# Moving every large tile of a two-layer diffusion block to SBUF addresses that are multiples of 1024 bytes

## The chip, the cores and the metric

The kernel runs on one core of a Trainium2 chip. Five engines work side by side: TensorE (matrix products; PE in the profile, with its loads of the stationary operand listed apart as PEld), VectorE (DVE), ScalarE (ACT), GpSimd (POOL) and SyncE (SP), whose queue issues all the DMAs here. On-chip memory, the SBUF, has 128 partitions; a tile is a block of up to 128 partitions and lies at the same byte address in each of them. The metric is the device time of one execution in microseconds (us); the kernel before takes 1386.08 us in the median of three runs.

## The reference

One latent stream `x` of 512 tokens and one context stream of 256 tokens, 1024 features each, go through two layers: differential attention, then a gated short convolution. Each is followed by a SwiGLU feed-forward block (FFN) with an inner width of 2816.

```
for i in range(2):
    sh1, sc1, g1, sh2, sc2, g2 = split(silu(c) @ ada_w[i] + ada_b[i], 6)
    h  = rmsnorm(x, norm1_g[i]) * (1 + sc1) + sh1
    y  = diff_attention(h, hc, ...) if i == 0 else short_conv(h, ...)
    x  = x + g1 * y
    h2 = rmsnorm(x, norm2_g[i]) * (1 + sc2) + sh2
    a, b = split(h2 @ ffn_w_in[i], 2)
    x  = x + g2 * ((silu(a) * b) @ ffn_w_out[i])
return rmsnorm(x, final_g)
```

In the attention each head has two softmax maps, of which the second is subtracted with a learned weight. Only the latent stream is returned, so of the context only what the first attention reads of it is computed.

## The kernel before

Features lie on the partitions and tokens on the free axis. A float32 product runs as three passes in float32r: each operand is split into a rounded part (hi) and the rest (lo), and hi*hi, hi*lo and lo*hi add up in PSUM. Those are the three lines of `mm3` (L78, L79, L80 in the profile), which nearly all products pass through:

```
nc.tensor.matmul(ps, sh, mh, start=start, stop=False)
nc.tensor.matmul(ps, sh, ml, start=False, stop=False)
nc.tensor.matmul(ps, sl, mh, start=False, stop=stop)
```

A matmul has a stationary operand (128 by 128, mostly a block of weights, loaded anew for each matmul) and a moving operand (mostly 512 or 256 columns of activations, 4 bytes each, so 2048 or 1024 bytes of every partition). `load_w` fetches 128x1024 of weights by DMA (`raw`), ScalarE casts the hi part (L54), VectorE subtracts it to get lo (L55). A tile of weights holds eight blocks of 512 bytes.

The order of work is that of the program's text, as a scheduler has merged it: the first norm and the first head's projections (to about 110 us); eight heads of attention, each beside the next one's projections (`attend`, `proj_qk_steps`, `proj_v_steps`; to about 460 us); the FFN of layer 0 (`ffn_in`, tiles pa and pb from h2; `out_gemm`, tile po_fo0 from U); the short convolution (psc, psu, psb from h1; po_so from Y); the FFN of layer 1 (pa and pb from h3; po_fo1 from U) and the last norm.

**Where tiles lie.** Pools are stacked from both ends of a partition. On the left `const` (small constants) begins at byte 1152 and ends at 5728; on it stand the pools `wp` and `wp2` (weights), `ap` (attention), `lp`, `up0`, `up1` (the FFN's inner values, tiles uh and ul) and `yp` (tiles yh and yl). Everything in them has a size that is a multiple of 1024 bytes, so the large tiles all begin at 608 modulo 1024, as 5728 does. On the right, pools go down from byte 229344, which is 992 modulo 1024: `hp` (the first norm's output, hh, hl, ch, cl), `h2p`, `h1p` and `h3p` (the later norms' outputs), `xtp` (the residual stream) and `op` (tiles o, later the last eight blocks of the first FFN's inner values, there called u). These large tiles begin at 992 modulo 1024. Both 608 and 992 are 32 modulo 64. One pool, `ap2`, lies above `ap` and its small tiles, at 192 modulo 1024; it holds ada, araw, qt, kt, rcos, rsin, sw and rt, which VectorE, ScalarE, GpSimd and DMAs use in the attention. A block of weights begins at 608 or 96 modulo 1024.

Of the kernel before, what the change touches and what calls it, by code (L numbers as in the profile page):

```python
# [11 lines left out]
F32 = mybir.dt.float32  # L12
# [4 lines left out]
PSUM = bass.MemoryType.PSUM  # L17

P = 128
# [5 lines left out]
def block_kernel(  # L25
# [6 lines left out]
    """Features on partitions, tokens on the free axis, from the first norm to the last.  # L32

    A float32 product runs as three float32r passes: each operand is split exactly into a part
    rounded to float32r (hi) and the rest (lo), and hi*hi + hi*lo + lo*hi accumulate in PSUM.
    """
# [27 lines left out]
    def load_w(src, name, dst=None):  # L64
        """[n*128, cols] of weights (n*cols <= 1024) as (hi, lo), each [128, n, cols]."""
        n, ncol = src.shape[0] // P, src.shape[1]
        w = n * ncol
        raw = wp.tile([P, 1024], F32, tag="raw", name=f"raw_{name}")
        nc.sync.dma_start(
            raw[:, :w].rearrange("p (k c) -> p k c", c=ncol),  # L70
            src.rearrange("(k p) c -> p k c", p=P),
        )
        return tuple(
            t[:, :w].rearrange("p (k c) -> p k c", c=ncol) for t in split_w(raw, w, name, dst)
        )
# [6 lines left out]
    def gemm_block(ps, ws, mov):  # L82
        """ps[128 outputs, tokens] = w.T @ mov; ws the tiles of w by rows, mov a list of (hi, lo) by block."""
        n, k = len(mov), 0
        for wh, wl in ws:
            for i in range(wh.shape[1]):
                mm3(ps, wh[:, i, :], wl[:, i, :], mov[k][0], mov[k][1], k == 0, k == n - 1)
                k += 1
# [4 lines left out]
    # ---------------------------------------------------------------- constants, small vectors  # L93
    st1 = const.tile([P, P], F32, name="st1")
    st2 = const.tile([P, P], F32, name="st2")
    nc.vector.memset(st1, 0.0)
    nc.vector.memset(st2, 0.0)
    rows = lambda v: v.rearrange("(j p) -> j p", p=P)
    nc.sync.dma_start(st1[0:8, :], rows(c[0]))
    nc.sync.dma_start(st1[8:16, :], rows(c_ctx))  # L100
    nc.sync.dma_start(st1[16:64, :], rows(ada_b[0]))
    nc.sync.dma_start(st1[64:72, :], rows(norm1_g[0]))
# [5 lines left out]
    nc.vector.tensor_copy(ones_r, ones_f)  # L108
    mhalf = const.tile([P, 8], F32, name="mhalf")
    nc.vector.memset(mhalf, -0.5)  # L110

    # ---------------------------------------------------------------- pools of the first layer
# [4 lines left out]
    # what the last head doesn't use any more, in a pool of its own  # L117
# [7 lines left out]
    # places: first what is done with when the next pools land on it  # L125
# [16 lines left out]

    def load_ada0(k, hf):
        """Columns of block k of the first norm's shift and scale, half of the rows: [4 blocks of rows][s][128]."""
        raw = wp.tile([P, 1024], F32, tag="raw", name=f"raw_a{k}_{hf}")
        rv = raw.rearrange("p (k s c) -> p k s c", s=2, c=P)
        for s in range(2):
            nc.sync.dma_start(
                rv[:, :, s, :],
                ada_w[0, hf * 512:(hf + 1) * 512, s * D + k * P:s * D + (k + 1) * P]  # L150
                .rearrange("(k p) c -> p k c", p=P),
            )
        return raw

    # streams in natural layout, by blocks of 128 tokens
# [18 lines left out]
    # silu of both conditioning vectors; as stationary columns (hi, lo) of each  # L174
# [11 lines left out]
    # ---------------------------------------------------------------- first norm  # L186
    def spread(r, n, tag, name):
        """Columns r[128 tokens, n] as [128, n*128] in PSUM, the same on every partition."""
        rh = ap.tile([P, 4], F32R, tag="rh", name=f"rh{name}")[:, :n]
        rl = ap.tile([P, 4], F32, tag="rl", name=f"rl{name}")[:, :n]  # L190
        nc.vector.tensor_copy(rh, r)
        nc.vector.tensor_tensor(rl, r, rh.bitcast(F32), op=ALU.subtract)
        ps = psB.tile([P, 512], F32, tag=tag, name=f"spr{name}")[:, :n * P]
        for i, q in enumerate((rh.bitcast(F32), rl)):
            dg = ap.tile([P, 4, P], F32R, tag=f"dg{i}", bufs=1, name=f"dg{i}{name}")[:, :n, :]
            nc.gpsimd.tensor_tensor(
                dg, ident[:, None, :].to_broadcast([P, n, P]), q[:, :, None].to_broadcast([P, n, P]),
                op=ALU.mult,
            )
            nc.tensor.matmul(ps, ones_r, dg.rearrange("p a b -> p (a b)"), start=(i == 0), stop=(i == 1))  # L200
        return ps

    def nat_rstd(src, tag, name):
        """1/rms of natural-layout tokens, spread over the partitions."""
# [27 lines left out]
    # modulation of the first norm, both streams: [block of D][shift, scale][latent, context]  # L232
# [28 lines left out]
    # the first group's values and the first head's queries and keys, block by block of the norms' output  # L261
# [25 lines left out]
    for k in range(DB):  # L287
# [12 lines left out]
        for t in range(TB):  # L300
            # two accumulations share a bank: the first one's start clears it for both
            mm3(
                vps[0][:, t * 256:(t + 1) * 256],
                hx[k][0][:, t * P:(t + 1) * P], hx[k][1][:, t * P:(t + 1) * P],
                wh[:, 256:512], wl[:, 256:512], k == 0 and t % 2 == 0, k == DB - 1 and t % 2 == 1,
            )
# [23 lines left out]
    # the other small vectors  # L330
# [15 lines left out]
    # lambda  # L346
# [9 lines left out]
    # ---------------------------------------------------------------- adaLN vectors on VectorE  # L356
    def ada_steps(l, j, pool, ps_pool, spread_sum):
        """mod[l][:, 8j:8j+8]: one modulation vector of the latent stream, in steps."""
        acc = pool.tile([P, D], F32, tag="ada", bufs=1, name=f"ada{l}_{j}")
        for k in range(DB):  # L360
# [3 lines left out]
            if not spread_sum:  # L364
                # VectorE is the busy one beside attention
# [21 lines left out]
        # sums over the partitions, on every partition; the diagonal blocks are the columns  # L387
# [21 lines left out]
    # ---------------------------------------------------------------- attention  # L409
# [18 lines left out]
    def halves_to(dst, src, both):  # L428
        """Moves a map's 64 rows of (hi, lo) where the score products want them."""
        for m in range(2):  # L430
            s = src[64 * m:64 * m + 64]
            for d in range(2):
                o = dst[m][64 * d:64 * d + 64]
                nc.sync.dma_start(
                    o.bitcast(F32), (s if both else s[:, d, :]).bitcast(F32)
                )

    def finish_q(h, ps):
        """Per map [hi; hi] and [lo; lo], the scores' scale (a power of two) folded in."""
# [7 lines left out]
    def finish_k(h, ps, psc):  # L447
        """Per map [hi; lo], latent keys first."""
# [55 lines left out]
    def attend(h, between, after=None):  # L504
# [4 lines left out]
        for pr in range(2):  # L509
# [6 lines left out]
            for s in range(2):  # L516
# [19 lines left out]
                # both maps over the first one's denominator, which the sub-norm takes up  # L536
# [26 lines left out]
    def subnorm(h, den, t0, t1):  # L563
        """O is den * o, so eps is scaled by den^2 under the root."""
# [18 lines left out]
    # first group and head: projected already  # L583
# [4 lines left out]
    # ---------------------------------------------------------------- norms and products after it  # L588
# [51 lines left out]
    def pair(pool, i, name):  # L640
        """(hi, lo) in place i of pool."""
# [3 lines left out]
    def wo_steps():  # L645
        """The first heads' part of the output projection, in the place of the norm's output."""
# [34 lines left out]
    for h in range(NH):  # L681
        # beside a head: the next one's queries and keys, part of the next group's values, or
        # the output projection
# [43 lines left out]
    def sqrt_ahead(k):  # L727
        """Has the square root's table loaded while the products before a norm still run."""
# [6 lines left out]
    class beside:  # L735
        """The second norm's first half runs beside the end of attention, in places of its early values."""
# [8 lines left out]
    # the FFN's first weights, in places of the first heads' outputs  # L745
# [12 lines left out]
    def out_gemm(src, mov, l, j, nlast, ps_pool, name, after):  # L758
        """XT += gate * (src.T @ mov); the last nlast blocks of outputs by halves of the tokens,
        each half followed by after(a, b)."""  # L760
# [51 lines left out]
    # the rest of the output projection, into the second norm  # L812
# [3 lines left out]
    # ---------------------------------------------------------------- FFN of layer 0  # L816
# [13 lines left out]
    # ---------------------------------------------------------------- layer 1: short convolution  # L830
# [32 lines left out]
    # ---------------------------------------------------------------- FFN of layer 1  # L863
# [5 lines left out]
    # ---------------------------------------------------------------- second product, final norm  # L869
# [7 lines left out]
    def gather(t, j):  # L877
        """Blocks of features back to natural layout: times the gain, and their squares' sum."""
# [31 lines left out]
    xt_pool.release()  # L910

# [6 lines left out]
def _rope_tables(n_tokens, head_dim=64, grid_w=64, base=10000.0):  # L918
    """cos and signed sin of the axial rotation, [128 rows of two maps, tokens]."""
# [36 lines left out]
```

## Time and profile before

| what | value |
|---|---|
| median of three runs | 1386.08 us (1384.31 to 1387.55) |
| profiled execution, span from first to last instruction | 1387.6 us |
| TensorE busy, matmuls | 1331.6 us, 96% of the span, 7052 matmuls |
| TensorE busy, weight loads | 1132.0 us, 82% |
| VectorE, ScalarE, GpSimd busy | 56%, 38%, 18% |
| DMA | 182.79 MB, mean 132 GB/s |

The page gives no time for the profiled execution other than its span, which lies 0.05 us above the slowest of the three runs; start and end outside the span can't be told from it. Matmuls overlap in the pipeline: the time shown for one (some 390 ns with 512 columns) is its own duration, and the next one starts long before it ends. The pace of a stretch is therefore read from starts, or from how many matmuls stand in a window, not from durations. A window's count takes in the matmuls that were still running at its left edge, one or two here.

### The profile page before, as it was taken

Reading aid. Unit: us, or ns where it says so; the run is one execution under the profiler, and the core shown is the slowest. Engines: PE = TensorE matmul, PEld = TensorE weight load, DVE = VectorE, ACT = ScalarE, POOL = GpSimd, SP = SyncE. Lnnn points to the kernel's source line nnn. Section 1 sums busy time; section 2 is a strip of 40 time slices with the busy share of each in tenths; the row PEclk is TensorE's granted clock in tenths of the full one; section 3 lists DMA queues with packets and bytes.
Section 4 is the critical chain, followed back from the end, with each engine's and each line's share of the span. In section 5 each row is a group of like instructions: output and inputs, shape, how many; then the busy total and the mean of one; then the engine's idle time right before and its main releaser. Section 6 shows DMA issues by size and latency. Waiting matters only on the chain.

```text
span 1387.6 us, 18007 instructions
## 1 busy us (share of the span) xinstructions
PE 1331.6 (96%) x7052; PEld 1132.0 (82%) x7052; DVE 778.7 (56%) x1043; ACT 529.7 (38%) x872; POOL 245.6 (18%) x197
## 2 busy tenths in 40 slices
PE   5989899899999999999999999999999999999997
PEld 4778799798888888888888889888898888888887
DVE  5886976777886776776742255444463333332222
ACT  6655556554455432333322244222352222222222
POOL 3244735514314100000001041000330000000000
PEclk9999999999999999999999999999999999999999
DMA  9857633623432666666643333332333333333321
GB/s 292 256 152 218 188 100 122 159 69 92 137 92 85 190 213 196 213 214 204 203 126 95 99 92 92 91 100 83 91 95 102 93 91 91 93 98 101 95 84 61
DMA packets 238742, 182.79 MB, mean 132 GB/s; under 512 B 6937, under 2 KB 220226, under 8 KB 238658
## 3 DMA queue, kind: packets, MB, share of 16 engines
q1 hardware_dynamic: 238658, 181.65, 44.6%
q8 instruction: 55, 0.90, 0.3%
q14 instruction: 29, 0.24, 0.1%
HBM read 162.75 MB, written 4.19 MB: 120 GB/s over the span
## 4 chain that ended last, share of the span: by engine, by line
PE 83%; DVE 8%; DMA 2%; ACT 2%; issue 2%; POOL 1%; SPq 0%; DVEq 0%; ACTq 0%; POOLq 0%
PE pb L78 6%; PE pb L79 6%; PE pb L80 6%; PE pa L78 6%; PE pa L80 6%; PE pa L79 6%; PE po_fo L78 6%; PE po_fo L79 6%; PE po_fo L80 6%; PE S L524 3%; PE psc L79 1%; PE pt L547 1%; PE psu L79 1%; PE psb L80 1%; PE psu L80 1%
## 5 line engine op out<-in xcount | busy, mean ns | idle before, releaser
L54 ACT CAST whi_f<-raw_f 128x1024 fp32r<-128x1024 f32 x87 | 91.2, 1049 | 249.7 <-issue 126.6
L55 DVE TENSOR_TENSOR wlo_f<-raw_f,whi_f 128x1024 fp32r<-128x1024 f32 x87 | 107.4, 1235 | 83.2 <-ACT whi_f L54 80.3
L55 DVE TENSOR_TENSOR wlo_fo<-raw_fo,whi_fo 128x1024 fp32r<-128x1024 f32 (+1 forms) x48 | 54.5, 1135 | 118.9 <-ACT whi_fo L54 117.3
L603 POOL TENSOR_TENSOR nacc<-nacc,nsq 128x256 f32<-128x256 f32 x30 | 30.6, 1020 | 503.4 <-ACT nsq L599 502.9
L78 PE MATMUL po_fo<-uh,whi_fo 128*128 128x512 f32 (+1 forms) x324 | 118.7, 366 | 0.1
L79 PE MATMUL po_fo<-ul,whi_fo 128*128 128x512 f32 (+1 forms) x324 | 118.6, 366 | 0.0
L80 PE MATMUL po_fo<-uh,wlo_fo 128*128 128x512 f32 (+1 forms) x324 | 118.4, 365 | 0.0
L54 ACT CAST whi_fo<-raw_fo 128x1024 fp32r<-128x1024 f32 (+1 forms) x48 | 47.1, 981 | 179.5 <-PE po_fo L79 143.2
L374 DVE SCALAR_TENSOR_TENSOR ada<-araw,sil,ada 128x1024 f32<-128x1024 f32 x49 | 62.9, 1284 | 38.2 <-DMA araw<-in_ada_w_dram 37.9
L799 DVE TENSOR_TENSOR uu<-sl,pb 128x512 f32<-128x512 f32 (+1 forms) x48 | 30.8, 641 | 87.3 <-PE pb L80 83.0
L532 ACT ACTIVATE e<-S,mx 128x768 f32<-128x768 f32 x64 | 57.8, 904 | 41.3 <-DVE mx L528 32.7
L80 PE MATMUL pb<-h2h,wlo_f 128*128 128x512 f32 (+1 forms) x192 | 72.5, 378 | 0.0
L78 PE MATMUL pa<-h3h,whi_f 128*128 128x512 f32 (+1 forms) x192 | 72.4, 378 | 0.0
L80 PE MATMUL pa<-h3h,wlo_f 128*128 128x512 f32 (+1 forms) x192 | 72.2, 376 | 0.0
L80 PE MATMUL pb<-h3h,wlo_f 128*128 128x512 f32 (+1 forms) x192 | 72.2, 376 | 0.0
L78 PE MATMUL pb<-h3h,whi_f 128*128 128x512 f32 (+1 forms) x192 | 72.2, 376 | 0.0
L79 PE MATMUL pb<-h3l,whi_f 128*128 128x512 f32 (+1 forms) x192 | 72.2, 376 | 0.0
L78 PE MATMUL pb<-h2h,whi_f 128*128 128x512 f32 (+1 forms) x192 | 72.2, 376 | 0.0
L79 PE MATMUL pb<-h2l,whi_f 128*128 128x512 f32 (+1 forms) x192 | 72.2, 376 | 0.0
L79 PE MATMUL pa<-h3l,whi_f 128*128 128x512 f32 (+1 forms) x192 | 72.1, 376 | 0.0
L528 DVE TENSOR_REDUCE mx<-S 128x1 f32<-128x768 f32 x64 | 60.2, 949 | 18.0 <-PE S L524 18.0
L78 PEld LDWEIGHTS po_fo<-uh,whi_fo 128*128 128x128 f32 x324 | 61.1, 189 | 10.5 <-DVE on L886 0.3
(362 smaller groups left out, 3727.2 us busy)
## 6 DMA issues: line engine op xcount, KB each, us to landing
raw_f<-in_ffn_w_in_dram SPq DMA_DIRECT2D x88, 512.0 KB, 3.8
araw<-in_ada_w_dram SPq DMA_DIRECT2D x80, 512.0 KB, 4.1
raw_fo<-in_ffn_w_out_dram SPq DMA_DIRECT2D x32, 512.0 KB, 3.7
raw_a<-in_ada_w_dram SPq DMA_DIRECT2D x32, 256.0 KB, 3.7
qs<-qt SPq DMA_DIRECT2D x32, 256.0 KB, 4.9
raw_wv<-in_da_wqkv_dram SPq DMA_DIRECT2D x12, 512.0 KB, 5.0
ks<-kt SPq DMA_DIRECT2D x32, 192.0 KB, 5.2
raw_fo<-in_ffn_w_out_dram SPq DMA_DIRECT2D x16, 384.0 KB, 4.2
```

What stands on the lines that cost most here:

```text
L54: nc.scalar.copy(hi, src)
L55: nc.vector.tensor_tensor(lo, src, hi.bitcast(F32), op=ALU.subtract)
L78: nc.tensor.matmul(ps, sh, mh, start=start, stop=False)
L79: nc.tensor.matmul(ps, sh, ml, start=False, stop=False)
L80: nc.tensor.matmul(ps, sl, mh, start=False, stop=stop)
L374: nc.vector.scalar_tensor_tensor(acc, raw, s, acc, op0=ALU.mult, op1=ALU.add)
L524: nc.tensor.matmul(S[:, a:b], q[m][:, j, qb * P:(qb + 1) * P], ks[m][:, a:b], start=(j == 0), stop=(j == 1),)
L528: nc.vector.tensor_reduce(out=mx[:, m:m + 1], in_=S[:, :KV], axis=AX.X, op=ALU.max, negate=True)
L532: nc.scalar.activation(em, S[:, :KV], AF.Exp, bias=mx[:, m:m + 1], accum_out=den[:, m, qb:qb + 1])
L547: nc.tensor.transpose(pt[:, i * P:(i + 1) * P], e[0][:, k * P:(k + 1) * P], ident)
L603: nc.gpsimd.tensor_tensor(acc, acc, sq, op=ALU.add)
L799: nc.vector.tensor_tensor(u, s, pb, op=ALU.mult)
```

## The change

The computation is untouched. Five edits in the layout:

- The two staging tiles `st1` and `st2` (512 bytes each) leave `const` and take the two places of the tag `ks1` in `ap`; their memsets and the DMAs that fill `st1` stand later in the text.
- A tile `pad` of 416 bytes, which nothing uses, joins `const`, so that it ends at byte 5120 = 5 * 1024. The left pools' large tiles thus begin at 0 modulo 1024.
- A pool `edge` of 992 bytes, which nothing uses, is the first on the right, so that the right pools go down from 228352 = 223 * 1024. Their large tiles begin at 0 modulo 1024, too.
- `ap2` moves along to 608 modulo 1024, which is 32 modulo 64 (it was 192, a multiple of 64).
- Docstrings and comments go, which changes line numbers and nothing else.

A block of weights now begins at 0 or 512 modulo 1024.

```diff
-    st1 = const.tile([P, P], F32, name="st1")
-    st2 = const.tile([P, P], F32, name="st2")
-    nc.vector.memset(st1, 0.0)
-    nc.vector.memset(st2, 0.0)
-    rows = lambda v: v.rearrange("(j p) -> j p", p=P)
-    nc.sync.dma_start(st1[0:8, :], rows(c[0]))
...
     nc.vector.tensor_copy(ones_r, ones_f)
+    const.tile([P, 104], F32, name="pad")
     mhalf = const.tile([P, 8], F32, name="mhalf")
...
+    edge = tc.alloc_tile_pool(name="edge", bufs=1, side="right")
+    edge.tile([P, 248], F32, name="edge")
     h_pool = tc.alloc_tile_pool(name="hp", bufs=1, side="right")
...
     xt_dram = nc.dram_tensor("xt_spill", [DB, P, T], F32, kind="Internal").ap()
 
+    rows = lambda v: v.rearrange("(j p) -> j p", p=P)
+    st1, st2 = (ap.tile([P, P], F32, tag=t, name=n) for t, n in (("ks1", "st1"), ("ks1", "st2")))
+    nc.vector.memset(st1, 0.0)
+    nc.vector.memset(st2, 0.0)
+    nc.sync.dma_start(st1[0:8, :], rows(c[0]))
...
     xt_pool.release()
+    edge.release()
```

TensorE, ScalarE and GpSimd execute the same instructions in the same order as before. Two places differ. The first is VectorE at the start of the program, where the zeroing of the staging tiles (st) stands ahead of that of two constants (ones_f, mhalf). Before:

```order
L952 UNCONDITIONAL_BRANCH
L96 MEMSET st_61 128x128
L97 MEMSET st_62 128x128
L106 MEMSET ones_f 128x128
L110 MEMSET mhalf 128x8
L108 CAST ones_r<-ones_f 128x128
L171 COPY V_189<-ps_V_190 128x128
L180 CAST cst<-sil 128x8 x2
```

After:

```order
L957 UNCONDITIONAL_BRANCH
L97 MEMSET ones_f 128x128
L102 MEMSET mhalf 128x8
L140 MEMSET st_168 128x128
L141 MEMSET st_169 128x128
L99 CAST ones_r<-ones_f 128x128
L175 COPY V_194<-ps_V_195 128x128
L184 CAST cst<-sil 128x8 x2
```

The two memsets of st have moved behind those of ones_f and mhalf; nothing else moves on VectorE. The second place is the SP queue where the second head's keys (ks) and queries (qs) are copied from their staging tiles (kt, qt); the waits are shown. Before:

```order
L434 DMA qs_0_1328<-qt_1325 64x1024 [waits DMAHW7_49,DVE_49]
L434 DMA qs_0_1328<-qt_1325 64x1024 [waits DMAHW0_49]
L434 DMA qs_1_1329<-qt_1325 64x1024 [waits DMAHW1_49,PE_49]
L434 DMA qs_1_1329<-qt_1325 64x1024 [waits DMAHW2_49]
L434 DMA ks_0_1396<-kt_1391 64x768 [waits DMAHW3_49,Activation_49]
L434 DMA ks_1_1397<-kt_1391 64x768 [waits DMAHW4_49]
L434 DMA ks_0_1396<-kt_1391 64x768 [waits DMAHW5_49,DVE_49]
L434 DMA ks_1_1397<-kt_1391 64x768 [waits DMAHW6_49]
```

After:

```order
L438 DMA qs_0_1333<-qt_1330 64x1024 [waits DMAHW7_49,DVE_49]
L438 DMA qs_0_1333<-qt_1330 64x1024 [waits DMAHW0_49]
L438 DMA qs_1_1334<-qt_1330 64x1024 [waits DMAHW1_49,PE_49]
L438 DMA qs_1_1334<-qt_1330 64x1024 [waits DMAHW2_49]
L438 DMA ks_0_1401<-kt_1396 64x768 [waits DMAHW3_49,Activation_49]
L438 DMA ks_1_1402<-kt_1396 64x768 [waits DMAHW4_49,PE_49]
L438 DMA ks_0_1401<-kt_1396 64x768 [waits DMAHW5_49,DVE_49]
L438 DMA ks_1_1402<-kt_1396 64x768 [waits DMAHW6_49]
```

The order is the same, and the first copy to the second map's keys now also waits for TensorE, since its place held `st2`, which a transpose reads.

## Rows read from the trace of the kernel before

**Rows 1.** The page: span, and busy time of each engine.
```profile
span 1387.6 us, 18007 instructions
PE 1331.6 (96%) x7052; PEld 1132.0 (82%) x7052; DVE 778.7 (56%) x1043; ACT 529.7 (38%) x872; POOL 245.6 (18%) x197
```

**Rows 2.** The page: the chain that ended last, by engine.
```profile
PE 83%; DVE 8%; DMA 2%; ACT 2%; issue 2%; POOL 1%; SPq 0%; DVEq 0%; ACTq 0%; POOLq 0%
```

**Rows 3.** Windows by stage: length; per engine busy us (x instructions); granted clock; DMA; GB/s.
```profile
0.00:110.00 110.00, 85.07 (x506) 67.70 (x506) 81.20 (x134) 64.16 (x106) 42.04 (x29) 0.92 0.78 233
110.00:462.00 352.00, 332.16 (x2129) 301.33 (x2130) 268.73 (x428) 188.44 (x365) 147.62 (x111) 0.96 0.45 124
462.00:1368.00 906.00, 902.63 (x4325) 751.94 (x4325) 420.73 (x463) 268.97 (x374) 55.90 (x58) 1.00 0.41 123
```

**Rows 4.** Lines by form, TensorE: shape, xcount | busy us, mean ns | idle before.
```profile
L78 PE MATMUL po_fo<-uh,whi_fo 128*128 128x512 f32 x252 | 98.1, 389 | 0.0
L78 PE MATMUL po_so<-yh,whi_so 128*128 128x512 f32 x40 | 15.6, 389 | 0.0
...
L78 PE MATMUL po_fo<-u,whi_fo 128*128 128x512 f32 x56 | 22.1, 395 | 0.0
L78 PE MATMUL pa<-h3h,whi_f 128*128 128x512 f32 x160 | 63.2, 395 | 0.0
L78 PE MATMUL psc<-h1h,whi_scc 128*128 128x512 f32 x48 | 18.9, 395 | 0.0
...
L524 PE MATMUL S<-ks,qs 128*128 128x512 f32 x128 | 43.9, 419 | 8.6 <-ACT e L532 5.5 <-DMA ks<-kt 3.1
L78 PE MATMUL psq<-hh,whi_wq 128*128 128x512 f32 x56 | 23.3, 417 | 0.2 <-ACT rtq L421 0.2
...
L78 PE MATMUL poa<-o,whi_woa 128*128 128x512 f32 x40 | 16.6, 415 | 2.9 <-ACT o L54 2.9
```

**Rows 5.** Windows, TensorE: first FFN product of layer 1, then its second.
```profile
1040.00:1250.00 210.00, 210.00 (x901) 1.00 0.33 95
1256.00:1355.00 99.00, 99.00 (x439) 1.00 0.31 88
```

**Rows 6.** Tile po_fo, 735 to 751 us: duration ns min/median/max, first and last start.
```profile
L78 PE MATMUL po_fo<-uh,whi_fo x16: 389/389/393, 735.1 to 750.9; 128*128 128x512 f32 x16
L78 PE MATMUL po_fo<-u,whi_fo x8: 392/394/398, 739.2 to 744.1; 128*128 128x512 f32 x8
```

**Rows 7.** Window of TensorE at 168 to 173 us.
```profile
168.00:173.00 5.00, 5.00 (x17) 0.50 0.90 244
```

**Rows 8.** Timeline, TensorE, at that clock: start us, us (two rows left out).
```profile
171.48 0.63 PE L79 MATMUL psq<-hl,whi_wq 128*128 128x512 f32 x1
...
172.76 0.63 PE L79 MATMUL psq<-hl,whi_wq 128*128 128x512 f32 x1
```

**Rows 9.** Timeline, TensorE, products of 256 columns (seven rows left out).
```profile
1372.11 0.28 PE L78 MATMUL po_fo<-uh,whi_fo 128*128 128x256 f32 x1
...
1373.07 0.28 PE L80 MATMUL po_fo<-uh,wlo_fo 128*128 128x256 f32 x1
```

**Rows 10.** Timeline, TensorE, 256 columns with four stationary columns (five rows left out).
```profile
61.89 0.28 PE L244 MATMUL pm<-whi_a,cst 128*4 128x256 f32 x1
...
62.57 0.28 PE L244 MATMUL pm<-whi_a,cst 128*4 128x256 f32 x1
```

**Rows 11.** Timeline of VectorE at the start: start us, us.
```profile
0.83 0.17 DVE L96 MEMSET st<- 128x128 f32 x1 [0.83 <-PEq L936]
...
1.23 0.07 DVE L110 MEMSET mhalf<- 128x8 f32 x1
```

**Rows 12.** Timeline of TensorE at the start.
```profile
7.90 0.69 PE L268 MATMUL ptx<-ident,xn 128*128 128x128 f32 x2 [3.10 <-DMA xn<-in_x_dram]
```

**Rows 13.** Tile ps_V: ns min/median/max, first and last start.
```profile
L170 PE MATMUL ps_V<-ident,st x2: 328/388/448, 4.4 to 75.3; 128*128 128x128 f32 x2
```

**Rows 14.** Tile ks, queue SP.
```profile
L434 SPq DMA_DIRECT2D ks<-kt x32: 461/588/1146, 104.4 to 371.3; - x32
```

More of the change, by code (lines that the diff above doesn't have):

```diff
@@ L91, in cut @@
         return [(h[:, a:b], l[:, a:b]) for h, l in mov]
-    st1 = const.tile([P, P], F32, name="st1")
-    st2 = const.tile([P, P], F32, name="st2")
-    nc.vector.memset(st1, 0.0)
-    nc.vector.memset(st2, 0.0)
-    rows = lambda v: v.rearrange("(j p) -> j p", p=P)
-    nc.sync.dma_start(st1[0:8, :], rows(c[0]))
-    nc.sync.dma_start(st1[8:16, :], rows(c_ctx))
-    nc.sync.dma_start(st1[16:64, :], rows(ada_b[0]))
-    nc.sync.dma_start(st1[64:72, :], rows(norm1_g[0]))
     ident = const.tile([P, P], F32, name="ident")
@@ L141, in block_kernel @@
     xt_dram = nc.dram_tensor("xt_spill", [DB, P, T], F32, kind="Internal").ap()
+    rows = lambda v: v.rearrange("(j p) -> j p", p=P)
[3 more added lines that the diff above has]
+    nc.sync.dma_start(st1[0:8, :], rows(c[0]))
+    nc.sync.dma_start(st1[8:16, :], rows(c_ctx))
+    nc.sync.dma_start(st1[16:64, :], rows(ada_b[0]))
+    nc.sync.dma_start(st1[64:72, :], rows(norm1_g[0]))
     def load_ada0(k, hf):
```

## The prediction, made before the changed kernel ran

> **What bounds the kernel now.** The page comes first. TensorE is busy for 1331.6 of 1387.6 us and no other engine for much more than half the span [rows 1], and the chain that ended last runs through TensorE for 83% of its length, through VectorE for 8%, DMAs for 2% [rows 2]. Next the windows by stage: from 462 to 1368 us TensorE stands idle for 3.4 of 906 us at full clock, while VectorE is busy for less than half of the time [rows 3]. There whatever shortens a matmul shortens the kernel. In the first 462 us it is different: TensorE is busy there too [rows 3], but the chain's TensorE share, 0.83 * 1387.6 = 1152 us, less the 903 after 462, leaves about 250 of the first 462 us, a little over half. I count half of a gain there.
>
> The view that decides is how fast matmuls follow each other. The clock is at its upper level, 2.4 GHz, in that stretch [rows 3], so 512 columns would take 213.3 ns at one column per cycle. Layer 1's first FFN product starts 901 matmuls in 210 us, less two that were running at the edge: 210/899 = 233.6 ns. Its second product starts 439 in 99 us: 99/437 = 226.5 ns [rows 5]. Each matmul thus costs 13 to 20 ns more than its columns. At 256 columns, eight steps take 0.96 us, 120 ns each instead of 106.7 [rows 9], the same surplus. At the lower clock level, 1.2 GHz [rows 7], three matmuls with 512 columns start 1.28 us apart, 427 ns each [rows 8], which is just 512 columns: no surplus. So the array doesn't set it. Something that feeds the array does, and it shows only when the array asks at full speed.
>
> The change speaks to that if the surplus depends on addresses, and the lines by form say that it does. The moving tiles uh and yh, on the left at 608 modulo 1024, have matmuls of 389 ns; h3, h1 and u, on the right at 992, have 395 [rows 4]. Lines L78 to L80, weights and shape are the same. The best comparison is inside one product: po_fo of layer 0 takes uh and u in turn within each block of outputs, with the same weights' tiles; uh has a median of 389 and u of 394 [rows 6]. The engine's other work is the same, so the few bits of the start address are what is left.
>
> **The change part by part.**
>
> *The left pools, 608 to 0 modulo 1024.* On the path after 462 us: po_fo<-uh, three lines of 252, and po_so<-yh, three lines of 40, 876 matmuls [rows 4], now 226.5 ns each.
>
> *The right pools, 992 to 0.* pa and pb, twelve groups of 160 (two products, two layers, three passes), psc, psu and psb, nine of 48, and po_fo<-u, three of 56: 2520 matmuls [rows 4], now about 233.5 ns.
>
> What does one cost that starts at 0? No tile here does. Below, the columns alone: 213.3 ns, as at the lower clock, where the time is the columns' alone [rows 8]. Above, 236 ns: the slow kind among the u matmuls lasts 398, 9 ns over uh's 389 [rows 6], 226.5 + 9. Two ways of carrying the rows on to 0: surplus 13.2 at 96 modulo 256 (608) and 20.2 at 224 modulo 256 (992) lie on a line that has 7.9 at 0, which is 221 ns; or the surplus comes from starting off a multiple of 64, which both do, and then it is gone. I take the middle, a surplus of 4, 217.5 ns, nearest to the uh rows among those that show a price. That saves 876 * 9 = 7.9 us and 2520 * 16 = 40.3 us.
>
> *256 columns.* Of 4325 matmuls after 462 us [rows 3], 3396 are those above and some 40 belong to sums, which leaves 890. They go from 119 or 120 ns to what they take where only four stationary columns are loaded, 0.68 us for six steps, 113 ns [rows 10]: 890 * 6 = 5.3 us. Between 106.7 and today's 120 this is the row in the middle.
>
> *The first 462 us.* The stretch from 110 us holds 2129 matmuls [rows 3]. S has 128 of 512 columns on the left; psq, psk (as many) and poa have 3 * 56 + 3 * 56 + 3 * 40 = 456 from the right [rows 4]. I put some 1240 at 256 columns; the rest are transposes and single columns. (584 * 15.5 + 1240 * 6) ns = 16.5 us, of which half, 8.2, is on the path. The first 110 us have 506 matmuls and wait for DMAs (share 0.78) [rows 3]: 1 us.
>
> *The weights and the other engines.* Loads of the stationary operand also move from 608 or 96 to 0 or 512. They overlap and their price is in the pace above; I give them none of their own. VectorE, ScalarE and DMAs have slack after 462 us [rows 3]; a gain there is hidden by TensorE. `ap2` goes the other way, to 32 modulo 64, but TensorE's long streams read nothing from it. Were its GpSimd and VectorE work 1% slower, half of 1% of the 147.6 and 268.7 us in [rows 3] would be 2 us.
>
> *Staging tiles and waits.* The memsets of st end about 0.2 us later, behind ones_f and mhalf [rows 11]. Queued behind them on SP are the DMAs into st1 and, after these, those of x. TensorE first waits for x itself, 3.1 us at 7.9 us [rows 12], so up to 0.2 us may be lost. The new wait of a ks copy is for the transpose of st2 at 75.3 us [rows 13], and the first ks copies start at 104.4 us [rows 14]: 29 us of cover, and behind it stand only copies of the same head. Nothing.
>
> Sum: 7.9 + 40.3 + 5.3 + 8.2 + 1 = 62.7, less 0.2, 62.5 us. The span of 1387.6 us lies 1.5 above the median of the runs, a tenth of a per cent; I take the gain from the median: 1386.1 - 62.5 = 1323.6, about 1324 us. With no surplus at all (213.3 and 106.7) the terms are 11.6 + 50.9 + 10.9 + 13.4 + 1.5 = 88, giving 1298; with 221 and 115 they are 4.8 + 31.5 + 3.6 + 6 + 0.7 = 47, giving 1339.
>
> The Trainium skill bears on this in TensorE: Matmul & The Clock Gate, section Back-to-back issue gap: an isolated matmul at full clock follows the last one after its columns plus 2.5 ns. The trace disagrees so far, with 13 to 20 ns. Were the whole difference due to addresses, an estimate by that page has 215.8 and 109.2 ns and a gain near 75 us, 1311 us.
>
> **The rivals.**
>
> *B, equal starts.* Surplus 13 belongs to each matmul with its weight load, wherever it starts, and only the excess on the right goes, because moving operand and weights then begin alike modulo 512, as uh and its weights already do. For it: 120 ns at 256 columns is the same 13 ns [rows 9]. Against it: with four stationary columns the surplus is 6.7, so the weight load isn't all of it [rows 10]. Then everything takes 226.5: 2520 * 7 = 17.6, and 456 * 7 / 2 = 1.6 in the attention: 19 us, 1367 us.
>
> *C, the change does nothing for TensorE.* Its reads don't care where a tile starts; left and right differ by what else goes on. Then the time is 1386 us. Against it stand uh and u inside one product [rows 6]. The Trainium skill's page SBUF — State Buffer, section Specifications (TRN2), speaks for C: it gives the memory lines of 16 bytes, and 608, 992 and 0 are all multiples of 16, so no read would touch more lines than now. By that rule uh and u should be alike, and the trace shows them 5 to 6 ns apart.
>
> *D, slower.* The run that starts 32 bytes below a multiple of 1024 lies almost where the new one will, and it is the slower of the two [rows 4]. If reading from a multiple of 1024 is the slow kind, every 512-column matmul takes 236: 876 * 9.5 + 2520 * 2.5 = 14.6 us, and (128 * 9.5 + 456 * 2.5)/2 = 1.2 us in the attention, so 1402 us. It decides from a pace of 231.7 ns on, where 876 * (p - 226.5) = 2520 * (233.5 - p). Against it: where both operands already begin alike modulo 512, the pace is the best [rows 5].
>
> **How the numbers follow.** My forecast (A), 0.50; B, 0.30; C, 0.09; D, 0.11. The predicted time is A's, 1324 us, with a range of its own of 1298 to 1339. A and B together hold 0.80, so the range reaches from 1304 (A's lowest corner needs every surplus gone at once) to 1378, which gives B room for a half of its gain. A difference of 0.2%, 2.8 us, is about what runs that spread by 3.2 us can tell. Faster is A and B, 0.80; same is most of C, 0.08; slower is D and the rest of C, 0.12.
>
> **What would show it.** The instruction counts and the order stay, so the starts are comparable one by one. A is right if the window of the second FFN product of layer 1 shows a pace between 213 and 222 ns and the first one the same; if po_fo<-u and po_fo<-uh have equal durations, near 380; and if 256 columns step by 107 to 115. B shows 226.5 in both windows and 120 unchanged; C the same two paces as now; D 232 or more in the second product. The attention's waits for ScalarE and DMAs should grow where TensorE arrives earlier; if they swallow more than half, the gain before 462 us is below 8 us. The forecast fails if the surplus is a property of loading 128 stationary columns rather than of addresses.

## The result, and the profile after

The changed kernel takes 1370.09 us (median of four runs, 1367.62 to 1371.09) against 1386.59 (1384.31 to 1387.55) for the kernel before on the same chip: ratio 0.9882, interval 0.9868 to 0.9896. That is faster by 16.5 us, 1.2%. The direction was forecast, but the gain was forecast at 62.5 us. The time lies in the stated range only because that was drawn to hold rival B as well: B, "equal starts", at 1367 us, comes nearest, and the experiments bear its relation out. The page's first lines and its chain, against [rows 1, 2]:

```profile
span 1368.1 us, 18008 instructions
PE 1312.1 (96%) x7052; PEld 1128.1 (82%) x7052; DVE 780.4 (57%) x1043; ACT 529.6 (39%) x872; POOL 244.8 (18%) x197
...
PE 79%; DVE 8%; DMA 4%; ACT 4%; issue 2%; POOL 2%; SPq 0%; DVEq 0%; ACTq 0%; POOLq 0%
```

TensorE's busy time fell by 19.5 us, which is the whole difference of the spans; the other engines kept theirs. TensorE still bounds the kernel; its share of the chain fell from 83% to 79%, and waits for DMAs and ScalarE took what it gave up. The windows of the same stages as [rows 3], and then the two FFN products of layer 1 as in [rows 5], which now lie earlier (length; per engine busy us and instructions; granted clock; DMA share; GB/s):

```profile
0.00:110.00 110.00, 85.73 (x515) 68.00 (x515) 81.19 (x134) 64.11 (x106) 43.12 (x30) 0.95 0.78 239
110.00:462.00 352.00, 331.73 (x2163) 301.78 (x2164) 273.88 (x433) 190.79 (x371) 147.07 (x111) 0.97 0.44 126
462.00:1368.00 906.00, 894.59 (x4377) 758.32 (x4375) 425.32 (x477) 274.72 (x396) 54.59 (x56) 1.00 0.41 124
1018.00:1235.00 217.00, 217.00 (x959) 179.78 (x958) 73.98 (x80) 62.30 (x80) 0.00 (x0) 1.00 0.34 102
1240.00:1339.00 99.00, 99.00 (x438) 82.06 (x437) 27.14 (x26) 21.04 (x22) 0.00 (x0) 1.00 0.29 85
```

The first product starts 959 matmuls in 217 us, less two at the edge: 226.8 ns instead of 233.6. The second starts 438 in 99 us: 227.1, what it took before within one matmul of the count. Right and left are alike now, and both have the pace that the left side had before. (The third window ends at the kernel's own end, hence 894.59 us.) The lines by form say the same of every product of [rows 4] after 462 us (shape, xcount | busy us, mean ns | idle before):

```profile
L78 PE MATMUL pa<-h3h,whi_f 128*128 128x512 f32 x160 | 62.3, 389 | 0.0
...
L78 PE MATMUL po_fo<-uh,whi_fo 128*128 128x512 f32 x252 | 98.1, 389 | 0.0
...
L78 PE MATMUL po_fo<-u,whi_fo 128*128 128x512 f32 x56 | 21.8, 390 | 0.0
...
L78 PE MATMUL psc<-h1h,whi_scc 128*128 128x512 f32 x48 | 18.7, 390 | 0.0
...
L78 PE MATMUL po_so<-yh,whi_so 128*128 128x512 f32 x40 | 15.6, 389 | 0.0
```

395 has become 389 or 390; 389 has stayed. The product in which u and uh alternate, against [rows 6] (duration ns min/median/max, first and last start), shows no difference between the two any more:

```profile
L78 PE MATMUL po_fo<-uh,whi_fo x16: 388/390/390, 724.8 to 740.4; 128*128 128x512 f32 x16
...
L78 PE MATMUL po_fo<-u,whi_fo x8: 389/390/390, 728.9 to 733.6; 128*128 128x512 f32 x8
```

And 256 columns, against [rows 9]: eight steps in 0.96 us, 120 ns, unchanged.

```profile
1352.24 0.28 PE L78 MATMUL po_fo<-uh,whi_fo 128*128 128x256 f32 x1
...
1353.20 0.28 PE L80 MATMUL po_fo<-uh,wlo_fo 128*128 128x256 f32 x1
```

By stage, from the first start of each to the first start of the next, the two traces differ like this (minus is faster):

| stage | matmuls of 512 columns from the right | before, us | after, us | difference |
|---|---|---|---|---|
| up to the first FFN | 584 of both sides | 442.8 | 437.3 | -5.5 |
| FFN of layer 0, first product, 512 columns | 960 | 228.9 | 224.6 | -4.3 |
| FFN of layer 0, second product, 512 columns | 168 | 107.1 | 105.7 | -1.4 |
| convolution, 512 columns | 432 | 100.4 | 98.0 | -2.4 |
| FFN of layer 1, first product, 512 columns | 960 | 224.0 | 217.6 | -6.4 |
| FFN of layer 1, second product, 512 columns | none | 104.7 | 104.7 | 0 |
| the convolution's output product, 512 columns | none | 27.2 | 27.2 | 0 |
| the six stretches of 256 columns | not counted | 144.1 | 144.6 | +0.5 |

Behind the first row, the stages with 512-column matmuls from the right gain, 14.5 us in all; those without do not. The traces' difference, 19.5 us, is 3 us more than that of the medians. The granted clock points at the first row for the excess: 0.92 and 0.96 in the first two windows before [rows 3], 0.95 and 0.97 after. The experiments come back to it.

In one place something was given back. The sums of the modulation (tile pada) run within the first product of layer 0's FFN, with a stationary tile of ones at 128 modulo 1024. By form, the kernel before:

```profile
L394 PE MATMUL pada<-adah,ones_r 128*128 128x512 f32 x14 | 5.6, 400 | 0.0
...
L394 PE MATMUL pada<-adal,ones_r 128*128 128x512 f32 x14 | 5.5, 391 | 0.0
```

and after:

```profile
L398 PE MATMUL pada<-adah,ones_r 128*128 128x512 f32 x14 | 5.7, 408 | 0.5 <-ACT adah L54 0.5
...
L398 PE MATMUL pada<-adal,ones_r 128*128 128x512 f32 x14 | 5.6, 399 | 0.0
```

They last 8 ns longer, and one now waits 0.5 us for ScalarE's cast. Why they last longer isn't shown: their starts differ from that of the ones by 224 modulo 256 before and by 128 after. That product gained 4.3 us and its twin in layer 1, which has no such sums, 6.4. The starts split the difference into two parts. Before, the product of layer 0 ran at 232.6 ns a matmul and not at 233.3, which left 0.7 us less to gain. After, it runs at 228.2 and not at 226.7, 1.5 us in all: about half is that wait, and the rest lies around the sums. Their own steps take up to 241 ns, and behind a pair of them nine steps of 223 to 237 ns pass before the matmuls settle at 225 to 228.

### The profile page after: what moved, and what is told of

It reads as the page before. It is cut to its first block, busy times and chain, and to the rows that moved or that the text cites. A ratio compares the mean times of both kernels' runs of the same rounds, so it can differ in the third digit from the quotient of the medians.

```text
span 1368.1 us, 18008 instructions
## 1 busy us (share of the span) xinstructions
PE 1312.1 (96%) x7052; PEld 1128.1 (82%) x7052; DVE 780.4 (57%) x1043; ACT 529.6 (39%) x872; POOL 244.8 (18%) x197
## 4 chain that ended last, share of the span: by engine, by line
PE 79%; DVE 8%; DMA 4%; ACT 4%; issue 2%; POOL 2%; SPq 0%; DVEq 0%; ACTq 0%; POOLq 0%
PE po_fo L78 6%; PE po_fo L79 6%; PE po_fo L80 6%; PE pb L79 5%; PE pb L78 5%; PE pb L80 5%; PE pa L78 5%; PE pa L79 5%; PE pa L80 5%; DMA araw<-in_ada_w_dram 3%; PE S L528 2%; PE psc L79 1%; PE psb L80 1%; PE psu L80 1%; PE psc L80 1%
## 5 line engine op out<-in xcount | busy, mean ns | idle before, releaser
L607 POOL TENSOR_TENSOR nacc<-nacc,nsq 128x256 f32<-128x256 f32 x30 | 30.7, 1023 | 494.1 <-ACT nsq L603 493.6
L803 DVE TENSOR_TENSOR uu<-sl,pb 128x512 f32<-128x512 f32 (+1 forms) x48 | 30.7, 640 | 81.5 <-PE pb L80 77.2
L79 PEld LDWEIGHTS po_fo<-ul,whi_fo 128*128 128x128 f32 x324 | 61.1, 189 | 9.9
```

Of the source, the lines that this page charges most:

```text
L607: nc.gpsimd.tensor_tensor(acc, acc, sq, op=ALU.add)
L803: nc.vector.tensor_tensor(u, s, pb, op=ALU.mult)
```

## The experiments

Two theories. R (relation): the pace depends on the difference between the starts of the moving and the stationary operand, modulo some power of two; before, the left pair differed by 0 modulo 512 and the right pair by 384. L (location): each operand's own start counts, and leaving 32 modulo 64, or reaching 1024, is what helped.

**Matmuls alone, every start modulo 512.** A kernel with nothing but one weight tile, one tile of activations and chains of 72 matmuls with hi and lo in `mm3`'s order; only starts and sizes change:

```diff
+    [(f"rel_{chr(97 + i)}", 32 * i, 0, 512, 128) for i in range(16)]
+    + [("abs_a", 32, 32, 512, 128), ("abs_b", 96, 96, 512, 128), ("abs_c", 480, 96, 512, 128), ("abs_d", 0, 128, 512, 128)]
+    + [("few_a", 0, 0, 512, 4), ("few_b", 384, 0, 512, 4)]
+    + [("half_a", 0, 0, 256, 128), ("half_b", 128, 0, 256, 128), ("half_c", 384, 0, 256, 128)]
+    + [("low_a", 0, 0, 512, 128), ("low_b", 32, 0, 512, 128), ("low_c", 384, 0, 512, 128)]
```

> A kernel with matmuls alone, 72 for each of 29 pairs of starts (moving operand, stationary operand); it computes nothing of the reference. Theory R (the pace depends on the difference of the two starts modulo 512): cases with equal starts (0 and 0, 32 and 32, 96 and 96) all at 227 ns; 480 against 96, and 384 against 0, alike at 232 to 234; 0 against 128 like them. Theory L (each operand's own place counts, multiples of 64 or more being cheap): equal starts at 32 and at 96 dearer than at 0; all differences that are multiples of 64 as cheap as 0. Both: with four stationary columns nearer to 220, with 2-byte elements near 216 whatever the start, since the surplus belongs to feeding 4 bytes an element.

Tiles by name (duration ns min/median/max, first and last start):

```profile
L54 PE MATMUL rel_a<-mov,sta x72: 388/390/390, 31.9 to 48.0; 128*128 128x512 f32 x72
L54 PE MATMUL rel_b<-mov,sta x72: 392/395/399, 48.2 to 64.8; 128*128 128x512 f32 x72
L54 PE MATMUL rel_c<-mov,sta x72: 388/392/397, 65.0 to 81.3; 128*128 128x512 f32 x72
L54 PE MATMUL rel_e<-mov,sta x72: 391/395/399, 98.3 to 114.9; 128*128 128x512 f32 x72
L54 PE MATMUL rel_i<-mov,sta x72: 388/390/398, 165.6 to 181.7; 128*128 128x512 f32 x72
L54 PE MATMUL abs_a<-mov,sta x72: 388/390/392, 299.3 to 315.4; 128*128 128x512 f32 x72
L54 PE MATMUL abs_b<-mov,sta x72: 386/390/397, 315.6 to 331.7; 128*128 128x512 f32 x72
L54 PE MATMUL abs_c<-mov,sta x72: 387/394/399, 332.0 to 348.5; 128*128 128x512 f32 x72
L54 PE MATMUL few_a<-mov,sta x72: 390/394/398, 365.6 to 382.0; 128*4 128x512 f32 x72
L54 PE MATMUL half_a<-mov,sta x72: 277/283/284, 398.9 to 407.4; 128*128 128x256 f32 x72
L54 PE MATMUL low_c<-mov,sta x70: 378/379/380, 455.7 to 471.0; 128*128 128x512 bf16 x70
```

The paces that follow are taken from the starts to the nanosecond, once the pace has settled. A change of starts disturbs the first steps: five of rel_i take 229 to 236 ns, ten of abs_b 223 to 237, and then both stay at 225 to 228. Differences of 0 and 256 bytes take 226.7 ns (rel_a, rel_i), 64 and 320 take 228.9 (rel_c), and the other multiples of 32 take 233.3, one of them 234.3. The sixteen values repeat after 256 bytes. Both operands at 32 or at 96 (abs_a, abs_b) take 226.7. The moving operand at 480 with weights at 96, 384 apart as on the right before, takes 233.3 (abs_c), and the moving operand at 0 with weights at 128 as much (abs_d). So R holds and L falls. The plainest pair has the moving operand at 32 each time: with the weights at 0 it takes 233.3 (rel_b), with the weights at 32 226.7 (abs_a). With four stationary columns equal starts and 384 apart take the same 231.7 ns (few_a, few_b). With 2-byte elements (low) the step is 215 to 216 ns at differences of 0, 32 and 384: no such surplus. But there the loads of the stationary operand are shorter, too, 98 ns against 188, so these cases don't tell which of the two operands matters.

**Equal starts without any alignment.** The kernel before, with 384 bytes ahead of the right pools, so that both sides begin at 608 modulo 1024, still 32 modulo 64:

```diff
+    edge = tc.alloc_tile_pool(name="edge", bufs=1, side="right")
+    edge.tile([P, 96], F32, name="edge")
...
+    edge.release()
```

> The kernel before, with the right pools alone moved down by 384 bytes, so that everything large lies at 608 modulo 1024: still 32 modulo 64, but equal on both sides. Theory R: the whole gain is there, 1370 us, pace 227 in all products. Theory L: no gain from it, 1386 us, or about 1378 if only the place close under a multiple of 1024 was bad.

1372.22 us (1371.0 to 1376.58), ratio 0.9886, interval 0.9861 to 0.9911. The lines by form:

```profile
L78 PE MATMUL po_fo<-uh,whi_fo 128*128 128x512 f32 x252 | 98.1, 389 | 0.0
L78 PE MATMUL pa<-h3h,whi_f 128*128 128x512 f32 x160 | 62.3, 389 | 0.0
```

The whole gain is there, within the intervals, with no large tile at a multiple of 64. A pool of 384 bytes does what five edits did.

**Alignment without equal starts.** The kernel after, with the right pools at 384 modulo 1024; everything lies at a multiple of 128:

```diff
-    edge.tile([P, 248], F32, name="edge")
+    edge.tile([P, 152], F32, name="edge")
```

> The changed kernel, with the right pools at 384 modulo 1024: everything large at multiples of 128, but the two sides 384 apart, as before. Theory R: the gain is lost for products from right-hand tiles, 1386 us with a pace of 232 to 234 there and 227 for left-hand ones. Theory L: as after, 1370 us.

1385.45 us (1384.2 to 1387.91), ratio 0.9983, interval 0.9972 to 0.9995: the gain is gone but for some 2 us. Right 395 again, left 390:

```profile
L78 PE MATMUL po_fo<-uh,whi_fo 128*128 128x512 f32 x252 | 98.2, 390 | 0.0
L78 PE MATMUL pa<-h3h,whi_f 128*128 128x512 f32 x160 | 63.2, 395 | 0.0
```

**The period.** The kernel after with `edge.tile([P, 184], ...)`: right at 256 modulo 1024, left at 0.

> The kernel after with 256 bytes less at the edge: the right pools begin at 256 modulo 1024, the left ones at 0. Theory R with a period of 256 bytes (as the matmuls alone showed): the right pace stays at 227 ns and the time at 1370 us. Theory R with a period of 512 bytes (how rival B of the prediction was worded, since blocks of weights begin 512 bytes apart): all 2520 matmuls on the right take 233.3, and the time is 1385 us, as with 384 bytes. The theory that 1024 itself matters: 1386 us.

1373.16 us (1369.67 to 1374.16), ratio 0.9902, interval 0.9876 to 0.9928, which overlaps that of the change. In the FFNs and the convolution all products of 512 columns last 389 or 390 ns on both sides; in the second product of layer 0 TensorE once waits 1.1 us for the cast of adah, against 0.5 us in the first product of the change. One of the lines by form:

```profile
L78 PE MATMUL pa<-h3h,whi_f 128*128 128x512 f32 x160 | 62.3, 389 | 0.0
```

So 256 bytes is the period in the kernel too, and 1024 has no part in it.

**Both sides apart.** The kernel after with its right pools 128 modulo 256 and, on the left, 128 unused bytes ahead of U and Y:

```diff
-    edge.tile([P, 248], F32, name="edge")
+    edge.tile([P, 216], F32, name="edge")
...
+    lp.tile([P, 32], F32, tag="shift", bufs=1, name="shift")
```

> The kernel after with its moving operands 128 modulo 256 on both sides and the weights at 0: on the right by 128 bytes less at the edge, on the left by a tile of 128 bytes that nothing uses, in front of U and Y. All moving operands of the FFNs and the convolution still begin at multiples of 128 bytes. Theory R: both sides now take 233.3 ns; against the kernel after the 2520 matmuls on the right lose 6.5 ns as in the kernel before (16 us in all), and the 876 on the left lose 6.5 ns too, 5.7 us; 256 columns win about 1.4 ns each, 890 times, 1.2 us. Together 1370 + 16 + 5.7 - 1.2 = 1391 us, slower than the kernel before by 0.3%. Theory that the left side is fast because it is the left side: 1385 us.

1392.47 us (1389.75 to 1395.57), ratio 1.0046, interval 1.003 to 1.0061: slower than before, as R said, and 22.4 us over the median of the change where 21 were expected. The left side takes the slow pace as soon as it differs from its weights:

```profile
L78 PE MATMUL po_fo<-uh,whi_fo 128*128 128x512 f32 x252 | 99.5, 395 | 0.0
L78 PE MATMUL pa<-h3h,whi_f 128*128 128x512 f32 x160 | 63.2, 395 | 0.0
```

The two FFN products of layer 1 in all six versions, from the first start of 512 columns to the last (960 and 462 matmuls):

| version | right minus weights, modulo 256 | left minus weights | first product, us (ns each) | second product, us (ns each) |
|---|---|---|---|---|
| before | 128 | 0 | 223.8 (233.3) | 104.5 (226.7) |
| the change | 0 | 0 | 217.4 (226.7) | 104.5 (226.7) |
| equal at 608 | 0 | 0 | 217.4 (226.7) | 104.5 (226.7) |
| right at 384 | 128 | 0 | 222.9 (232.4) | 104.5 (226.8) |
| right at 256 | 0 | 0 | 217.4 (226.7) | 104.5 (226.7) |
| both apart | 128 | 128 | 223.8 (233.3) | 107.6 (233.3) |

The difference sets the pace to within a nanosecond, no closer. At 128 it is 233.3 ns in this product and 232.4 in the convolution before, and 232.4 and 233.3 with the right at 384. What chooses between the two is open.

The same traces tell what the first row of the stage table is worth. In these profiled executions the first FFN begins 5.5, 5.3, 3.0, 3.9 and 3.4 us earlier than in that of before, in the table's order, and it begins 3.4 us earlier even where everything is apart. The granted clock differs as well. In the first 462 us the trace of before has 47.8 us at the lower level, 1.2 GHz; the others have 30.7, 34.1, 41.0, 37.6 and 34.1 us. At that level a matmul of 512 columns takes 427 ns [rows 8] and not some 230, so 17 us less of it are worth up to 8 us (an estimate), and most of the 5.5 us can be the clock's. "Equal at 608" and "both apart" have the same 34.1 us, and between these two the first FFN begins 1.9 us earlier with equal starts, near B's 1.6; it is one pair of executions, an indication and no measurement. A run's time lies some 1.7 us above its span (1369.84 and 1368.1 for the change), so the profiled execution of before, with a span of 1387.6, took about 1389 us and was 3 us slower than its median.

**What the remaining 13.3 ns belong to.** Matmuls alone again, 72 of a kind: the moving operand 0 to 28 bytes past the weights, fewer stationary columns, other lengths.

```diff
+    + [(f"fine_{chr(97 + i)}", 4 * i, 0, 512, 128) for i in range(8)]
+    + [(f"cols_{chr(97 + i)}", 0, 0, 512, m) for i, m in enumerate((8, 16, 32, 64, 96, 112, 120, 124))]
+    + [(f"colsoff_{chr(97 + i)}", 128, 0, 512, m) for i, m in enumerate((32, 64, 96))]
+    + [(f"len_{chr(97 + i)}", 0, 0, n, 128) for i, n in enumerate((288, 320, 384, 448, 496))]
+    + [(f"lenoff_{chr(97 + i)}", 128, 0, n, 128) for i, n in enumerate((288, 320, 384, 448, 496))]
```

> Matmuls alone, 72 of a kind one after the other; the reference's output is not computed. fine: 512 columns with the moving operand 0, 4, ... 28 bytes past the stationary one. cols: 512 columns with 8 to 124 stationary columns, at equal starts; colsoff: 32, 64 and 96 stationary columns, moving operand 128 bytes past. len: 288 to 496 moving columns at equal starts; lenoff: the same 128 bytes past. Theory 'per matmul': a matmul costs its columns at 2.4 GHz plus 13.3 ns at equal starts and 20 ns where the starts differ modulo 256, whatever its size: 133.3, 146.7, 173.3, 200 and 220 ns for len, 6.7 ns more for lenoff. Theory 'per column': the surplus is a share of the columns, 6.25% at equal starts, and 9.4% apart, so 127.5, 141.7, 170.0, 198.4 and 219.6 ns for len. Theory 'weight load': the 13.3 ns come with loading 128 stationary columns and shrink with fewer, so cols falls towards 213.3 at 8 columns; against it stood 231.7 at 4 columns. Theory 'exact equality': fine shows 226.7 at 0 bytes alone and 233.3 from 4 bytes on; its rival, 'lines of 32 bytes': 226.7 up to 28 bytes.

```profile
L54 PE MATMUL fine_f<-mov,sta x72: 399/404/404, 116.5 to 133.5; 128*128 128x512 f32 x72
L54 PE MATMUL fine_h<-mov,sta x72: 387/387/391, 150.6 to 166.7; 128*128 128x512 f32 x72
...
L54 PE MATMUL cols_d<-mov,sta x72: 387/390/398, 216.9 to 233.2; 128*64 128x512 f32 x72
...
L54 PE MATMUL len_b<-mov,sta x72: 304/309/309, 359.0 to 369.4; 128*128 128x320 f32 x72
L54 PE MATMUL len_d<-mov,sta x72: 362/368/368, 382.1 to 396.7; 128*128 128x448 f32 x72
```

None of the theories holds. Neither exact equality nor lines of 32 bytes: 4, 8, 12, 16, 20, 24 and 28 bytes past take 236.7, 233.3, 228.9, 231.7, 240.0, 233.3 and 226.7 ns. Not the amount of weights loaded: 8 to 124 stationary columns at equal starts take 228.3 to 233.4 ns, all above the 226.7 of 128. With 32 and 64 stationary columns, starts 128 apart are no slower than equal ones (230.8 against 231.7 and 229.4 against 230.0), with 96 they are (231.7 against 230.0). Neither a fixed price nor a share of the columns: at equal starts 288, 320, 384, 448 and 496 columns take 131.7, 146.7, 173.3, 206.7 and 223.3 ns, which is 11.7, 13.3, 13.3, 20 and 16.7 over their columns at 2.4 GHz; 128 bytes apart it is 133.3, 146.7, 176.0, 204.0 and 223.3. So starts apart cost something at 384 and 512 columns, nothing at 320 and 496, and at 448 they are the faster ones.

**Is any start better?** The other multiples of 4 bytes within 256, 48 matmuls each, and 256 columns at the multiples of 32:

```diff
+    + [(f"g_{'abcdefg'[i // 8 - 1]}{'abcdefgh'[i % 8]}", 4 * i, 0, 512, 128) for i in range(9, 64) if i % 8]
+    + [(f"half_{chr(97 + i)}", 32 * i, 0, 256, 128) for i in range(8)]
```

> Matmuls alone, 48 of a kind one after the other; the reference's output is not computed. g: 512 columns, the moving operand begins 36 to 252 bytes past a multiple of 256, in steps of 4 bytes and without the multiples of 32, which are known; the stationary operand begins at a multiple of 512. half: 256 columns, 0, 32, ... 224 bytes past. The question is whether any start is better than an equal one (226.7 ns; 120 ns at 256 columns). Theory 'equal is best': no kind of g is below 226.7. Theory 'each difference has its own pattern of meetings between the two reads', by the irregular 229 to 240 ns between 4 and 24 bytes: paces spread between about 220 and 240, some below 226.7, and a version of the kernel with such a difference would be faster than the kernel after by 3396 times what is below. half: 118.5 to 120 ns throughout, so nothing to win.

```profile
L51 PE MATMUL g_cb<-mov,sta x48: 398/403/406, 183.4 to 194.7; 128*128 128x512 f32 x48
...
L51 PE MATMUL g_cd<-mov,sta x48: 387/387/392, 206.1 to 216.8; 128*128 128x512 f32 x48
...
L51 PE MATMUL half_b<-mov,sta x48: 278/280/284, 581.4 to 587.0; 128*128 128x256 f32 x48
```

All lie between 226.7 ns (0, 28, 60, 108, 156 and 252 bytes past) and 240.0 (20, 100, 132, 196 and 244). None beats an equal start, so, by R, no placement makes the kernel faster at 512 columns. At 256 columns the starts apart are better or level, 117.8 to 120.0 against 120.0; the most that could bring is an estimated 890 * 2.2 ns = 2 us, which no run here shows; the same tiles also feed the 512 columns.

## Why the forecast was wrong

The direction held: part of the surplus over 213.3 ns depends on addresses, it sits in TensorE's pace after 462 us, and the stages without matmuls from the right did not move. Rival C, whose argument rested on memory lines of 16 bytes (the Trainium skill, SBUF — State Buffer, section Specifications (TRN2)), falls with it: starts that are all multiples of 128 differ by 6.6 ns.

The step that failed is "What does one cost that starts at 0?". Both ways of carrying the rows on, the line through 96 and 224 modulo 256 and "off a multiple of 64", took the surplus for a property of the moving operand's own start. It belongs to the difference from the weights' start. By that the rows already held the answer: on the left, moving operand and weights differed by 0 modulo 256 before and after, and so the left pace of [rows 5], 226.5 ns, was the price of the new place on both sides. "I give them none of their own", of the weights, was the same slip once more: the change moved the weights along with the left pools, so nothing changed between them. A start at 0 was thus put at 217.5 ns and measured 226.7: nothing saved on the left instead of 9 ns a matmul, 6.6 ns or less on the right instead of 16.

B had the relation right, but not all of its reasons. The period is 256 bytes and not 512, and the 13 ns that it gave to "each matmul with its weight load" are no fixed price: they are 11.7 to 20 ns by length, and fewer stationary columns don't lower them at 512 columns.

Term by term:

- Left pools, forecast 7.9 us: measured 0 (104.5 us for the second product in both traces).
- Right pools, forecast 40.3: measured 14.5, the four gaining stages. B's term was 17.6, by 7 ns each; before, the pace on the right was 233.3 in layer 1, but 232.6 in layer 0's product and 232.4 in the convolution, and after, pada gave some of it back.
- 256 columns, forecast 5.3: measured -0.5. The row taken for the middle, 113 ns with four stationary columns [rows 10], was no guide to what a start at 0 brings with 128 of them, which is 120 ns alone, too. At 512 columns, matmuls alone with four stationary columns take 231.7 ns, more than with 128; at 256 columns this was not tried. The row had also been the argument against B.
- The first 462 us, forecast 9.2 with the first 110: 5.5 in the traces, most of which can be the granted clock's; the one pair with equal time at 1.2 GHz differs by 1.9.
- The staging tiles, forecast -0.2: TensorE's first wait for x ends at 7.64 us instead of 7.90 [rows 12], so no loss shows. The ks copies start at 102.2 us instead of 104.4 [rows 14]; no cost of their new wait shows.

Of the check named at the end of the prediction, every sign came out as B's: 226.8 and 227.1 ns in both windows, 120 ns at 256 columns. D's sign was 232 or more. D's fear is real in another form: what lies 128 apart from its weights is slow on the left, too, and when both sides do, the kernel takes 22 us more than the change.

The estimate by the Trainium skill (TensorE: Matmul & The Clock Gate, section Back-to-back issue gap, columns plus 2.5 ns for an isolated matmul, so 215.8) is met by 2-byte elements, 215 to 216 ns, at the three differences tried. With the 4-byte elements of this kernel no start comes within 10 ns of it.

What stays open is why a 4-byte matmul keeps 13.3 ns at equal starts. The Trainium skill (TensorE: Matmul & The Clock Gate, section Step-by-step: what each phase is for) gives the engine two independent read ports, so that loading the next weights takes no bandwidth from the running matmul. By that one would not expect the place of the weights to matter; here it does, by 6.6 ns (rel_b and abs_a). That the reads of the moving operand and of the next weights meet somewhere with a period of 256 bytes would fit the dependence on their difference, but no run here shows such a meeting itself, and none has matmuls that keep their weights loaded.

## What to carry to other kernels

When a pace differs between tiles, compare the addresses of all operands of the instruction, not only those of the one that stands out: here the difference modulo 256 bytes between moving and stationary operand decides, with 4-byte elements, 512 columns and 128 stationary columns, and one unused pool of 384 bytes gives the whole gain (ratio 0.9886 against 0.9882). Before you carry a cost on to a place that no row shows, ask whether some row already shows that place under another description. And where a layout puts pools at both ends of memory, work out both ends modulo 256: a size at either end that is no multiple of 256 sets the relation for every product whose operands lie on both sides.

## What the hardware showed unexpectedly

- The pace at full clock, 512 columns of 4 bytes and 128 stationary columns: 226.7 ns where the starts differ by 0 modulo 256 bytes, 228.9 at 64, 233.3 to 234.3 at the other multiples of 32, and up to 240.0 at other multiples of 4.
- Fewer stationary columns don't help: 4 to 124 take 228.3 to 233.4 ns at equal starts. With 4, 32 and 64 of them, starts apart are no slower than equal ones.
- The pace takes some matmuls to settle after a change of starts: ten steps of 223 to 237 ns in abs_b before it stays at 225 to 228.
- Lengths are not equal in it: 320 columns 146.7 ns (13.3 over), 448 columns 206.7 (20 over), 512 columns 226.7 (13.3 over).
- At 256 columns equal starts and 96 apart are the slowest of the multiples of 32, 120.0 ns, with 117.8 the best; at 512 columns equal starts are the best.
- 2-byte elements: 215 to 216 ns at differences of 0, 32 and 384 bytes, with loads of the stationary operand of 98 ns instead of 188.
